# Scores of two column blocks in one two-bank PSUM piece, and the roots of the variances moved into the attention pairs

## The chip, the cores and the metric

The kernel runs on one core of one Trainium2 chip. The metric is the device time of one execution in microseconds (us). A core has a matrix engine (TensorE, rows named PE, and PEld for its weight loads), a vector engine (VectorE, DVE), a scalar engine (ScalarE, ACT), GpSimd (POOL) and SyncE (SP), which in this kernel issues every DMA. Each engine has a program of its own and works it off in the order in which it stands; engines meet at semaphores. PSUM, which takes the matmul results, has eight banks of 128 x 512 fp32 numbers.

## What is computed

One layer of an encoder is applied to 16 meta tokens with 512 prompt tokens and 1024 sample tokens (1552 columns in all, 1536 of them tokens). The lines that matter here:

```python
u = rms_norm(h, pre_g)
z = jnp.einsum('bld,de->ble', u, w_in.astype(u.dtype))
c_val, c_glu, c_gate, q, k, v, a_gate = jnp.split(z, [...], axis=-1)
conv_out = conv_module(c_val, c_glu, conv_w, conv_b, ln_g, ln_b) * jax.nn.silu(c_gate)
o_meta, o_grid = neighbourhood_attention(q[:, N_META:], k[:, N_META:], v[:, N_META:],
                                         q[:, :N_META], k[:, :N_META], v[:, :N_META], rel_bias)
att = jnp.concatenate([o_meta, o_grid], axis=1).reshape(B, L, D_ATT) * jax.nn.silu(a_gate)
mixed = jnp.concatenate([conv_out, att], axis=-1)
y = jnp.einsum('ble,ed->bld', mixed, w_out.astype(mixed.dtype))
return h + rms_norm(y, post_g)
```

`conv_module` ends in a layer norm over the 1024 channels of a token: `y = xc * lax.rsqrt(var + LN_EPS) * g + b`, and a silu. In the attention every query sees a window of 8 rows x 16 columns of the grid and the meta tokens: scores plus a relative bias, softmax, weighted values.

## The kernel before

Every matmul with weights is done three times, on a high and a low part of each operand (`hi`/`lo`, `qh`/`ql`, `kh`/`kl`, `mh`/`ml`). A scheduler inside the build sets the final order of each engine's program from the code's data flow; `tc.issue_after(x)` puts what stands in it behind `x`.

**Until about 660 us** the kernel normalises the tokens, projects values, gates and conv inputs, and runs the depthwise convolution, whose result goes to DRAM as `zs`.

**The attention** runs over 8 pairs of heads, 3 groups of token rows (`g`) and 2 halves (`hf`), so 48 steps of four column blocks `j` each: 192 blocks. In one turn of the loop `scores(p, g, hf)` stands for the step itself, `transposes` for the step before, `weighted` for the one before that, and `between` puts in a projection (`pair_proj`, `pair_q`, or in the last pair pieces of `a_gate`), 24 matmuls a piece into tiles `mm`. For a block `scores` has three matmuls into a tile `ss` (one PSUM bank of two, pool `ps_s`); VectorE adds the bias and takes the maximum out of it (L585, into `pt`), ScalarE takes the exponential (L589), VectorE the reciprocal and the scaling (L590, L591). `transposes` turns `pt` over on the matrix engine (`tp`, L600) and ScalarE copies it out (`pT`, L602); `weighted` sums the values into `po` (L616).

**Beside it** `statistics()` takes one call per step: it reads `zs`, and stores mean and variance of every token's 1024 channels to the DRAM tensor `std`. `roots()` then loads the 1536 variances into `rv` (128 x 12, L675), ScalarE takes the root (L676), VectorE the reciprocal (L677), and L678 stores them back, number by number:

```python
    s = std[1:2]
    var = bass.AP(s.tensor, s.offset, [[1, 128], [128, TG // 128]])
    nc.sync.dma_start(rv, var)
```

**The end:** `a_gate(6, 7)` (six pieces of 24 matmuls, copied out to `ag` by L342), then `mix(t, part)` makes the inputs of the last product for 128 tokens: part 0 loads mean and root (`mb`, L752), subtracts and multiplies on VectorE (L764, L765), silu on ScalarE (L767), times the silu of the gate (L768, L769), `mh` and `ml` (L770, L771); part 1 does the same for the attention. `load_wo` brings 16 chunks of the output weights (L735) and splits them (ScalarE L745, VectorE L746). `product` (L792) multiplies into `py`; tiles t = 0 and t = 1 are done together, part 0 of both first.

In the code before, `roots()` and the first `mix` stand behind the last pair:

```python
    with tc.issue_after(last_pt[0]):
        roots()
        mix(0, (0,))
```

Of the kernel before, what the change touches and what calls it, by code (L numbers as in the profile page):

```python
# [10 lines left out]
F32 = mybir.dt.float32  # L11
F32R = mybir.dt.float32r
AF = mybir.ActivationFunctionType
# [19 lines left out]
GR = (  # L33
    dict(R=9, k3=(0, 11, 0), k2=(0, 16, 0), vrow=0),
    dict(R=12, k3=(8, 12, 0), k2=(8, 16, 0), vrow=8),
    dict(R=13, k3=(13, 13, 0), k2=(10, 16, 3), vrow=13),
)
# [40 lines left out]
BMM, BSS, BTP = 3, 2, 2  # L78
# [15 lines left out]
def tile_encoder(ctx: ExitStack, tc: tile.TileContext, mt, xn, w_main, w_v, wo, cw, cb, lg, lb, pg, postg, rbt, rmask, y):  # L94
    nc = tc.nc
# [9 lines left out]
    const = ctx.enter_context(tc.tile_pool(name="const", bufs=1))  # L105
    es_ps = ExitStack()
    ps_mm = es_ps.enter_context(tc.tile_pool(name="ps_mm", bufs=BMM, space=bass.MemoryType.PSUM))
    ps_s = es_ps.enter_context(tc.tile_pool(name="ps_s", bufs=BSS, space=bass.MemoryType.PSUM))
    ps_t = es_ps.enter_context(tc.tile_pool(name="ps_t", bufs=BTP, space=bass.MemoryType.PSUM))
    ps_o = es_ps.enter_context(tc.tile_pool(name="ps_o", bufs=1, space=bass.MemoryType.PSUM))  # L110

    ones = const.tile([128, 128], F32, name="ones")
    nc.vector.memset(ones, 1.0 / D)
    eps_sb = const.tile([128, 3], F32, name="eps_sb")
# [4 lines left out]
    rv = const.tile([128, TG // 128], F32, name="rv")  # L119
# [311 lines left out]


    es2 = ExitStack()
    kpool = es2.enter_context(tc.tile_pool(name="kpool", bufs=1, side="right", reuse_waits="tile"))
    qpool = es2.enter_context(tc.tile_pool(name="qpool", bufs=1, side="right", reuse_waits="tile"))

# [14 lines left out]
    last = [None]  # L451
# [31 lines left out]
    last_qk = [None]  # L483
# [59 lines left out]
    def block(g, j):  # L543

        e = ebufs[g][{0: 1, 7: 2}.get(j, 0)]
        if g == 0:
            return min(max(j - 1, 0), 5), 3, "k3", 2, 108, e
        R8 = GR[g]["R"] * 8
        if j in (0, 7):
            return min(j, 6), 2, "k2", 2, R8, e  # L550
        return j - 1, 3, "k3", 3, R8, e

    def load_values(p, g):
        esl = slice(p * 128, p * 128 + 128)
        R8 = GR[g]["R"] * 8
        if g == 0:
            vt = apool.tile([108, 2, 6, 128], F32, name="vp", bufs=VPB)
            for ch, p0, b0, k0, n in ((0, 0, 0, 0, 72), (0, 72, 1, 0, 36), (1, 0, 1, 36, 36), (1, 36, 2, 0, 72)):
                nc.sync.dma_start(vt[p0:p0 + n, ch], vd[b0:b0 + 6, k0:k0 + n, esl].rearrange("b k e -> k b e"))
        else:  # L560
            vt = apool.tile([104, 8, 128], F32, name="vt", bufs=2)
            nc.sync.dma_start(vt[:R8], vd[:, GR[g]["vrow"] * 8:GR[g]["vrow"] * 8 + R8, esl].rearrange("b k e -> k b e"))
        vts[p, g] = vt

    def scores(p, g, hf):
        if hf == 0:
            load_values(p, g)
        kh, kl = kbufs[p]
        qh, ql = qbuf.pop((p, g, hf))
        R8 = GR[g]["R"] * 8  # L570
        for jj in range(4):
            j = hf * 4 + jj
            b0, nk, key, _, _, e = block(g, j)
            ra, rn, ro = GR[g][key]
            w = rn * 8
            ss = ps_s.tile([128, 512], F32, name="ss")
            for i, (q, k) in enumerate(((qh, kh), (qh, kl), (ql, kh))):
                last_qk[0] = nc.tensor.matmul(ss[:, :nk * w], lhsT=q[:, jj].rearrange("p h x -> p (h x)"),  # L578
                                 rhs=k[:, b0:b0 + nk, ra:ra + rn, :].rearrange("p b r c -> p b (r c)"),
                                 start=(i == 0), stop=(i == 2))  # L580
            sv_ = ss[:, :nk * w].rearrange("p (k x) -> p k x", k=nk)[:, :, ro * 8:ro * 8 + R8]
            pt = apool.tile([128, 312], F32, name="pt", bufs=PTB)
            pv = pt[:, :nk * R8]
            sm = apool.tile([128, 4], F32, name="sm", bufs=8)
            nc.vector.tensor_tensor_reduce(out=pv.rearrange("p (k x) -> p k x", k=nk), in0=sv_,  # L585
                                           in1=e.rearrange("p k r c -> p k (r c)"), scale=1.0,
                                           scalar=-3.0e38, op0=ALU.add, op1=ALU.max, accum_out=sm[:, 0:1])
            nc.vector.tensor_scalar(out=sm[:, 1:2], in0=sm[:, 0:1], scalar1=-1.0, scalar2=None, op0=ALU.mult)  # L588
            last[0] = nc.scalar.activation(out=pv, in_=pv, func=AF.Exp, bias=sm[:, 1:2], scale=1.0, accum_out=sm[:, 2:3])  # L589
            nc.vector.reciprocal(sm[:, 3:4], sm[:, 2:3])  # L590
            nc.vector.tensor_scalar(out=pv, in0=pv, scalar1=sm[:, 3:4], scalar2=None, op0=ALU.mult)  # L591
            pts[p, g, j] = pv
# [55 lines left out]
    def statistics():  # L648
        for t in range(TG // 128):
            tsl = slice(t * 128, t * 128 + 128)  # L650
            hx = []
            for k in range(2):
                x = gpool.tile([128, 512], F32, name="ag", tag="ag", bufs=2).rearrange("p (c t) -> p c t", c=8)
                a = t % 4 * 128 + k * 64
                nc.sync.dma_start(x, zs[t // 4][:, :, a:a + 64].rearrange("c p t -> p c t"))
                hx.append((x, slice(k * 64, k * 64 + 64)))
            yield
            for moment in range(2):
                for x, sl in hx:
                    nc.vector.tensor_reduce(out=ms[:, sl], in_=x.rearrange("p c t -> p t c"), op=ALU.add, axis=mybir.AxisListType.X)  # L660
                yield
                ps = new_mm()
                with tc.issue_after(last_mm[0]):
                    nc.tensor.matmul(ps[:, :128], lhsT=ones, rhs=ms, start=True, stop=True)
                nc.scalar.copy(out=row[0:1], in_=ps[0:1, :128])
                nc.sync.dma_start(std[moment:moment + 1, tsl], row[0:1])
                if moment == 0:
                    for x, sl in hx:
                        nc.vector.tensor_tensor(out=x, in0=x, in1=ps[:, sl].unsqueeze(1).broadcast_to([128, 8, 64]), op=ALU.subtract)
                        nc.scalar.activation(out=x, in_=x, func=AF.Square)  # L670

    def roots():
        s = std[1:2]
        var = bass.AP(s.tensor, s.offset, [[1, 128], [128, TG // 128]])
        nc.sync.dma_start(rv, var)  # L675
        nc.scalar.activation(out=rv, in_=rv, func=AF.Sqrt, bias=eps_sb[:, 1:2])  # L676
        nc.vector.reciprocal(rv, rv)  # L677
        nc.sync.dma_start(var, rv)  # L678

    stats = statistics()  # L680
    knext, last_pv, last_pt = [None], [None], [None]
# [2 lines left out]
    for n in range(len(groups) + 2):  # L684
        if n < len(groups):
            p, g, hf = groups[n]
# [67 lines left out]
    def mix(t, parts=(0, 1)):  # L754
        for part in parts:
            if part == 0:
                moments(t)
            mx, gt = mxs[part], gts[part]
            mh, ml = [x[t % 2 * 2 + part] for x in (mhs, mls)]
            g, csl = t // 4, slice(t % 4 * 128, t % 4 * 128 + 128)  # L760
            nc.sync.dma_start(mx, (zs, mad)[part][g][:, :, csl].rearrange("c p t -> p c t"))
            nc.sync.dma_start(gt, (cgd, agd)[part][g][:, :, csl].rearrange("c p t -> p c t"))
            if part == 0:
                nc.vector.tensor_tensor(out=mx, in0=mx, in1=mb[:, 0:1].broadcast_to([128, 8, 128]), op=ALU.subtract)  # L764
                nc.vector.tensor_tensor(out=mx, in0=mx, in1=mb[:, 1:2].broadcast_to([128, 8, 128]), op=ALU.mult)  # L765
                for c in range(8):
                    nc.scalar.activation(out=mx[:, c], in_=mx[:, c], func=AF.Silu, scale=lg_sb[:, c:c + 1], bias=lb_sb[:, c:c + 1])  # L767
            nc.scalar.activation(out=gt, in_=gt, func=AF.Silu)  # L768
            nc.vector.tensor_tensor(out=mx, in0=mx, in1=gt, op=ALU.mult)  # L769
            nc.scalar.copy(out=mh, in_=mx)  # L770
            (nc.vector if t < MLT else nc.gpsimd).tensor_tensor(out=ml, in0=mx, in1=mh.bitcast(F32), op=ALU.subtract)  # L771

    with tc.issue_after(last_pt[0]):
        roots()
        mix(0, (0,))
    for n in range(16):
        if n == 6:
# [132 lines left out]
```

## Time and profile before

| | |
|---|---|
| median of 3 runs | 1466.19 us (1464.93 to 4892.21) |
| the profiled execution | 1466.53 us, its span 1464.5 us |
| granted TensorE clock, mean | 0.996 of full speed |
| PE busy | 1436.8 us (98%) |
| DVE, ACT, POOL busy | 1014.2, 562.7, 256.6 us |

The span runs from the first to the last instruction; the execution's own time is 2.0 us longer. Times below are counted from the span's start. A matmul's end is modelled, so the distance from the start of one to the start of the next says more than its length.

### The profile page before, as it was taken

To read this page: it belongs to the slowest core of one execution; us is meant where nothing else is said; L and a number is where in the kernel's file an instruction comes from. 1 tells how busy PE (TensorE), PEld (TensorE's weight loads), DVE (VectorE), ACT (ScalarE), POOL (GpSimd) and SP (SyncE) were. 2 spreads that over 40 slices of the span, in tenths; PEclk is the share of its full clock that TensorE was granted. 3 is DMA by queue.
4 is the path that set the end of the run, shared out by engine and by line. 5 is a ranking of instruction groups with operands and counts; after the bars stand their busy time and mean duration, and the time that the engine had idled before them with its cause. 6 is when DMAs were issued, how large, how long until landed. Compare 5 with 4: busy or idle time off the path is not lost.

```text
span 1464.5 us, 24133 instructions
## 1 busy us (share of the span) xinstructions
PE 1436.8 (98%) x9536; PEld 1238.6 (85%) x9536; DVE 1014.2 (69%) x1739; ACT 562.7 (38%) x1298; POOL 256.6 (18%) x188
## 2 busy tenths in 40 slices
PE   7999999999999999999999999999999889999998
PEld 6988998988998888888888988988888768888886
DVE  6599999998999899836776777767543265332431
ACT  7311111112111111235565555655544465455440
POOL 2042022113101211222111111121110002122120
PEclk9999999999999999999999999999999989999999
DMA  8113113313231212242332232323232594545531
GB/s 267 42 47 118 47 55 110 93 40 91 74 97 51 88 59 87 94 116 65 87 88 80 69 98 77 88 79 89 72 93 81 130 312 135 167 122 148 160 107 43
DMA packets 153464, 145.19 MB, mean 99 GB/s; under 512 B 37216, under 2 KB 125432, under 8 KB 153352
## 3 DMA queue, kind: packets, MB, share of 16 engines
q1 hardware_dynamic: 153352, 143.67, 33.0%
q8 instruction: 74, 1.21, 0.3%
q14 instruction: 38, 0.31, 0.1%
HBM read 105.35 MB, written 42.72 MB: 101 GB/s over the span
## 4 chain that ended last, share of the span: by engine, by line
PE 92%; DMA 3%; ACT 2%; DVE 1%; POOL 1%; issue 1%; SPq 0%; DVEq 0%; ACTq 0%; POOLq 0%
PE mm L180 37%; PE py L792 18%; PE tp L180 9%; PE mm L322 5%; PE ss L578 5%; PE po L180 5%; PE po L616 4%; PE tp L600 4%; PE tp L322 3%; PE po L322 1%; POOL vl L142 1%; DMA std<-rv 1%; DMA yo<-in_wo 0%; ACT mx L767 0%; DMA wraw<-in_wo 0%
## 5 line engine op out<-in xcount | busy, mean ns | idle before, releaser
L180 PE MATMUL mm<-uw,whi 128*128 128x512 f32 (+2 forms) x1904 | 560.1, 371 | 3.3 <-ACT ag L342 3.3
L272 DVE SCALAR_TENSOR_TENSOR z<-ub,cw_sb,z 128x1536 f32<-128x1536 f32 (+2 forms) x270 | 498.7, 1853 | 8.1
L180 PEld LDWEIGHTS mm<-uw,whi 128*128 128x128 f32 x1904 | 341.8, 188 | 59.2 <-ACT ag L342 4.3
L180 PE MATMUL mm<-uw,wlo 128*128 128x512 f32 (+2 forms) x952 | 352.4, 370 | 1.1 <-POOL wlo L142 1.1
L142 POOL TENSOR_TENSOR wlo<-wraw,whi 128x1024 fp32r<-128x1024 f32 x48 | 130.5, 2720 | 524.3 <-ACT whi L141 500.3
L180 PEld LDWEIGHTS mm<-uw,wlo 128*128 128x128 f32 x952 | 179.0, 188 | 27.2 <-POOL wlo L142 1.4
L792 PE MATMUL py<-uw,mh 128*128 128x512 f32 x576 | 181.8, 397 | 0.0
L180 PE MATMUL tp<-uw,whi 128*128 128x512 f32 (+2 forms) x512 | 132.9, 344 | 0.0
L792 PEld LDWEIGHTS py<-uw,mh 128*128 128x128 f32 x576 | 108.7, 189 | 25.7
L589 ACT ACTIVATE pt<-pt,sm 128x216 f32<-128x216 f32 (+4 forms) x192 | 97.3, 507 | 80.3 <-DVE sm L588 70.3
L792 PE MATMUL py<-uw,ml 128*128 128x512 f32 x288 | 113.7, 396 | 0.0
L602 ACT COPY pT<-tp 108x256 f32<-108x256 f32 (+4 forms) x192 | 78.3, 420 | 84.5 <-PE tp L600 55.4
L764 DVE TENSOR_TENSOR mx<-mx,mb 128x1024 f32<-128x1024 f32 x12 | 14.7, 1225 | 123.2 <-DMA mx<-zs 107.8
L180 PEld LDWEIGHTS tp<-uw,whi 128*128 128x128 f32 x512 | 89.3, 188 | 11.6
L585 DVE CUSTOM_DVE_ANT_0 pt<-ss,ei 128x216 f32<-128x216 f32 (+2 forms) x144 | 62.6, 437 | 46.3 <-PE tp L600 22.7
L180 PE MATMUL tp<-uw,wlo 128*128 128x512 f32 (+2 forms) x256 | 88.1, 344 | 0.0
L771 POOL TENSOR_TENSOR ml<-mx,mh 128x1024 fp32r<-128x1024 f32 x20 | 48.4, 2443 | 224.2 <-ACT mh L770 224.2
L600 PE MATMUL tp<-ident,pt 128*96 128x128 f32 (+2 forms) x480 | 85.5, 275 | 0.3 <-ACT pT L602 0.2
L322 PE MATMUL mm<-vh,uw 128*128 128x256 f32 x448 | 83.5, 285 | 0.7 <-DVE uw L208 0.4
L591 DVE TENSOR_SCALAR pt<-pt,sm 128x216 f32<-128x216 f32 (+4 forms) x192 | 72.1, 375 | 4.9
L141 ACT CAST whi<-wraw 128x1024 fp32r<-128x1024 f32 x48 | 50.3, 1048 | 61.4 <-DMA wraw<-in_w_main 17.8
L180 PE MATMUL po<-uw,whi 128*128 128x512 f32 (+2 forms) x272 | 72.9, 347 | 0.0
(170 smaller groups left out, 2175.7 us busy)
## 6 DMA issues: line engine op xcount, KB each, us to landing
wraw<-in_w_main SPq DMA_DIRECT2D x48, 512.0 KB
xt<-in_xn SPq DMA_DIRECT2D x12, 512.0 KB
vd<-vs SPq DMA_DIRECT2D x96, 64.0 KB
zs<-zc SPq DMA_DIRECT2D x24, 256.0 KB
cgd<-ag SPq DMA_DIRECT2D x24, 256.0 KB
agd<-ag SPq DMA_DIRECT2D x24, 256.0 KB
ag<-zs SPq DMA_DIRECT2D x24, 256.0 KB
mad<-mo SPq DMA_DIRECT2D x24, 256.0 KB
```

Of the source, the lines that this page charges most:

```text
L142: eng.tensor_tensor(out=lo, in0=raw, in1=hi.bitcast(F32), op=ALU.subtract)
L180: last_mm[0] = nc.tensor.matmul(ps[:, :n], lhsT=w[:, dc, :], rhs=u[dc // 4][:, dc % 4, :], start=(dc == 0 and i == 0), stop=(dc == DC - 1 ...
L272: nc.vector.scalar_tensor_tensor(out=zv, in0=ub[:, a:b, k:k + 512], scalar=cw_sb[:, c, k:k + 1], in1=zv, op0=ALU.mult, op1=ALU.add)
L322: nc.tensor.matmul(ps[:, :256], lhsT=u[dc // 4][:, dc % 4, :], rhs=w[dc // 4][:, dc % 4, :], start=(dc == 0 and i == 0), stop=(dc == DC - ...
L578: last_qk[0] = nc.tensor.matmul(ss[:, :nk * w], lhsT=q[:, jj].rearrange("p h x -> p (h x)"), rhs=k[:, b0:b0 + nk, ra:ra + rn, :].rearrange ...
L585: nc.vector.tensor_tensor_reduce(out=pv.rearrange("p (k x) -> p k x", k=nk), in0=sv_, in1=e.rearrange("p k r c -> p k (r c)"), scale=1.0, ...
L589: last[0] = nc.scalar.activation(out=pv, in_=pv, func=AF.Exp, bias=sm[:, 1:2], scale=1.0, accum_out=sm[:, 2:3])
L591: nc.vector.tensor_scalar(out=pv, in0=pv, scalar1=sm[:, 3:4], scalar2=None, op0=ALU.mult)
L600: nc.tensor.transpose(out=tp[:kt, k * 128:k * 128 + 128], in_=pv[:, k * kt:k * kt + kt], identity=ident)
L602: last_pt[0] = nc.scalar.copy(out=pT[:kt, :nt * 128], in_=tp[:kt, :nt * 128]).ins
L616: last_pv[0] = nc.tensor.matmul(po[hs, j, :], lhsT=v, rhs=pT[:kt, k * 128 + h * 64:k * 128 + h * 64 + 64], start=(k == 0), stop=(k == nt - ...
L792: nc.tensor.matmul(pss[hf], lhsT=m[e // 8][:, e % 8], rhs=w[e][:, hf * 512:hf * 512 + 512], start=(n == 0 and i == 0), stop=(n == 15 and i ...
```

## The change

The two-bank pool `ps_s` is closed before the attention, and a pool `ps_ss` with a single piece of two banks takes its place. For every second block six matmuls fill both halves of the piece `sss`, first all of block j, then all of block j + 1; what follows for each block is as before. The next six wait until the piece has been read. The work of `roots()` goes to the end of `statistics()`: its load of `rv` is issued when the last variances are stored, in the seventh pair; the root comes two steps later, behind the exponential that was issued last there; the reciprocal and the store follow. `mix(0, (0,))` stays where it is in the code.

```diff
-    ps_s = es_ps.enter_context(tc.tile_pool(name="ps_s", bufs=BSS, space=bass.MemoryType.PSUM))
...
+    es_st = ExitStack()
+    ps_s = es_st.enter_context(tc.tile_pool(name="ps_s", bufs=BSS, space=bass.MemoryType.PSUM, reuse_waits="tile"))
...
+    es_st.close()
+    ps_ss = es_ps.enter_context(tc.tile_pool(name="ps_ss", bufs=1, space=bass.MemoryType.PSUM, reuse_waits="tile"))
...
+            if jj % 2 == 0:
+                sss = ps_ss.tile([128, 2, 512], F32, name="sss")
+                for y in range(2):
+                    b0, nk, key, _, _, e = block(g, j + y)
+                    ra, rn, ro = GR[g][key]
+                    for i, (q, k) in enumerate(((qh, kh), (qh, kl), (ql, kh))):
+                        last_qk[0] = nc.tensor.matmul(sss[:, y, :nk * rn * 8], lhsT=q[:, jj + y].rearrange("p h x -> p (h x)"),
+                                                      rhs=k[:, b0:b0 + nk, ra:ra + rn, :].rearrange("p b r c -> p b (r c)"),
+                                                      start=(i == 0), stop=(i == 2))
...
-            ss = ps_s.tile([128, 512], F32, name="ss")
-            for i, (q, k) in enumerate(((qh, kh), (qh, kl), (ql, kh))):
-                last_qk[0] = nc.tensor.matmul(ss[:, :nk * w], lhsT=q[:, jj].rearrange("p h x -> p (h x)"),
-                                 rhs=k[:, b0:b0 + nk, ra:ra + rn, :].rearrange("p b r c -> p b (r c)"),
-                                 start=(i == 0), stop=(i == 2))
+            ss = sss[:, jj % 2]
...
-    def roots():
         s = std[1:2]
         var = bass.AP(s.tensor, s.offset, [[1, 128], [128, TG // 128]])
         nc.sync.dma_start(rv, var)
-        nc.scalar.activation(out=rv, in_=rv, func=AF.Sqrt, bias=eps_sb[:, 1:2])
+        yield
+        yield
+        with tc.issue_after(last[0].ins):
+            nc.scalar.activation(out=rv, in_=rv, func=AF.Sqrt, bias=eps_sb[:, 1:2])
         nc.vector.reciprocal(rv, rv)
         nc.sync.dma_start(var, rv)
+        yield
...
     with tc.issue_after(last_pt[0]):
-        roots()
         mix(0, (0,))
```

The orders below are those of the built programs; line numbers of the changed kernel are a little higher than those of before (there L688 is the store of `rv`, L763 the load of `mb`, L775 and L776 the two steps of `mix` on VectorE, L593 to L599 the softmax, L582 the scores).

SyncE's DMA issues behind the last pair in the kernel before, where the roots are stored (`mad` and `agd` are stores of attention and gate, `xr` and `yo` take output weights):

```order
L343 DMA agd_68<-ag 128x512 [waits Activation_49]
L678 DMA std<-rv 128x12x1 [waits DMAHW1_49,DVE_49]
L621 DMA mad_65<-mo 128x512 [waits DMAHW2_49,DVE_49]
L752 DMA mb<-std 128x2x128 [waits DMAHW3_49,DMAHW1_49]
L735 DMA wraw<-in_wo 128x1024 [waits DMAHW4_49,Pool_49]
L735 DMA xr<-in_wo 128x1024 [waits DMAHW5_49,PE_49]
L735 DMA yo<-in_wo 128x1024 [waits DMAHW6_49,DMAHW2_49]
```

In the changed kernel these issues stand at the start of the eighth pair, ahead of the next gate's weights (`wraw<-in_w_main`) and of values (`vt`):

```order
L565 DMA vt<-vd 96x8x128 [waits DMAHW6_49,PE_49]
L629 DMA mad_64<-mo 128x512 [waits DMAHW7_49,DVE_49]
L688 DMA std<-rv 128x12x1 [waits DMAHW0_49,DVE_49]
L344 DMA agd_66<-ag 128x512 [waits DMAHW1_49,Activation_49]
L763 DMA mb<-std 128x2x128 [waits DMAHW2_49,DMAHW0_49]
L763 DMA mb<-std 128x2x128 [waits DMAHW3_49,DMAHW2_49,DVE_49]
L157 DMA wraw<-in_w_main 128x1024 [waits DMAHW4_49,Pool_49]
L565 DMA vt<-vd 104x8x128 [waits DMAHW5_49,PE_49]
```

The store of the roots and the first two loads of `mb` moved forward from behind the attention to the first steps of the eighth pair.

VectorE in the kernel before, at the same place of the program, behind the last softmax:

```order
L591 TENSOR_SCALAR pt<-pt,sm 128x208 [waits DVE_49]
L620 COPY mo<-po 128x512 [waits DMAHW0_49,PE_49]
L677 RECIPROCAL rv<-rv 128x12 [waits Activation_49]
L620 COPY mo<-po 128x512 [waits DMAHW6_49,DVE_49,PE_49]
L764 TENSOR_TENSOR mx<-mx,mb 128x1024 [waits DMAHW3_49]
L746 TENSOR_TENSOR wol_12185<-wraw,woh_12184 128x1024 [waits DMAHW4_49,Activation_49]
L765 TENSOR_TENSOR mx<-mx,mb 128x1024 [waits DVE_49]
```

VectorE in the changed kernel, from the last softmax of the seventh pair (216 columns: first blocks of the eighth):

```order
L599 TENSOR_SCALAR pt<-pt,sm 128x208 [waits DVE_49]
L687 RECIPROCAL rv<-rv 128x12 [waits Activation_49]
L593 ISA pt,sm<-sss,e_5367 128x216 [waits PE_49,Pool_49]
L593 ISA sm 128x1
L593 ISA pt,sm<-sss,ei_5366 128x216 [waits Pool_49]
L593 ISA sm 128x1
L596 TENSOR_SCALAR sm<-sm 128x1 [waits DVE_49] x2
L775 TENSOR_TENSOR mx<-mx,mb 128x1024 [waits DMAHW4_49,DMAHW2_49]
L598 RECIPROCAL sm<-sm 128x1 [waits Activation_49] x2
L776 TENSOR_TENSOR mx<-mx,mb 128x1024 [waits DVE_49]
L599 TENSOR_SCALAR pt<-pt,sm 128x216 [waits DVE_49] x2
L593 ISA pt,sm<-sss,ei_5366 128x216 [waits PE_49]
```

L775, which waits for `mx` and for `mb` (DMAHW2), moved between the first two blocks' maxima and the reads of the third and fourth block of the eighth pair.

The matrix engine in the kernel before, at the start of the eighth pair (264 columns) behind the last scores of the seventh (256):

```order
L578 MATMUL ss<-kh,ql_5357 128x256
L616 MATMUL po<-pT,vt 64x64 x22
L578 MATMUL ss<-kh,qh_5180 128x264 [waits DVE_49]
L578 MATMUL ss<-kl,qh_5180 128x264
L578 MATMUL ss<-kh,ql_5181 128x264
L578 MATMUL ss<-kh,qh_5180 128x264 [waits DVE_49]
L578 MATMUL ss<-kl,qh_5180 128x264
L600 MATMUL tp<-ident,pt 104x128 [waits Activation_49]
L600 MATMUL tp<-ident,pt 104x128 x2
L578 MATMUL ss<-kh,ql_5181 128x264
L180 MATMUL mm<-uw,whi 128x512
```

The matrix engine in the changed kernel, from the end of the second run of six of the eighth pair to the start of the third:

```order
L582 MATMUL sss<-kl,qh_5184 128x264
L582 MATMUL sss<-kh,ql_5185 128x264
L624 MATMUL po<-pT,vt 64x64 [waits DMAHW1_49]
L624 MATMUL po<-pT,vt 64x64 x21
L181 MATMUL mm<-uw,wlo 128x512
L181 MATMUL mm<-uw,whi 128x512
L582 MATMUL sss<-kh,qh_5190 128x264 [waits DVE_49,PE_49]
L582 MATMUL sss<-kl,qh_5190 128x264
L608 MATMUL tp<-ident,pt 104x128 [waits Activation_49]
```

Scores come in runs of six on one wait, where before each block of three waited for a bank of its own. Between the end of the first run of the eighth pair and the start of the third the changed program has 20 matmuls of a projection, 6 transposes, the 6 of the second run and 22 of `po`. In the whole attention it has the same 3598 matmuls; 14 of the 95 distances from one run of six to the next hold less than 1.5 us of other matmuls (at the distances from start to start of rows 8).

## Rows read from the trace of the kernel before

**Rows 1.** The page, busy time of each engine, share of the span, instructions.
```profile
PE 1436.8 (98%) x9536; PEld 1238.6 (85%) x9536; DVE 1014.2 (69%) x1739; ACT 562.7 (38%) x1298; POOL 256.6 (18%) x188
```

**Rows 2.** Waits of PE in the attention: total us, times, longest.
```profile
PE po L616 <- ACT pT L602: 0.5, 1, 0.5
PE tp L600 <- ACT pT L602: 0.2, 1, 0.2
```

**Rows 3.** Waits of PE from 1143 us to the end.
```profile
PE py L792 <- ACT mh L770: 4.6, 1, 4.6
PE mm L180 <- ACT ag L342: 3.3, 1, 3.3
PE py L792 <- ACT ag L342: 1.8, 1, 1.8
```

**Rows 4.** Windows: from:to, length, PE busy (matmuls), granted clock, DMA share, GB/s.
```profile
660.00:1142.00 482.00, 481.63 (x4338) 1.00 0.29 81
1142.00:1206.00 64.00, 53.92 (x222) 0.92 0.85 246
1202.00:1206.00 4.00, 4.00 (x11) 0.51 0.92 270
1206.00:1446.00 240.00, 240.00 (x1032) 1.00 0.45 134
```

**Rows 5.** Timeline of SyncE's issues: start, us, engine, line, what, [idle].
```profile
1144.28 0.37 SPq L678 DMA_DIRECT2D std<-rv  x1
1144.86 0.56 SPq L621 DMA_DIRECT2D mad<-mo  x1
1154.83 0.37 SPq L752 DMA_DIRECT2D mb<-std  x1
1155.29 0.42 SPq L735 DMA_DIRECT2D wraw<-in_wo  x1
```

**Rows 6.** Timeline of DVE behind the attention; in brackets idle time before, what ended it.
```profile
1144.03 0.23 DVE L677 RECIPROCAL rv<-rv 128x12 f32<-128x12 f32 x1 [15.05 <-ACT rv L676]
...
1160.17 1.23 DVE L764 TENSOR_TENSOR mx<-mx,mb 128x1024 f32<-128x1024 f32 x1 [15.34 <-DMA mb<-std]
1161.32 1.22 DVE L746 TENSOR_TENSOR wol<-wraw,woh 128x1024 fp32r<-128x1024 f32 x1
```

**Rows 7.** Timeline of ACT behind the attention.
```profile
1142.40 1.28 ACT L676 ACT_TABLE_LOAD   x1
1143.69 0.30 ACT L676 ACTIVATE rv<-rv,eps_sb 128x12 f32<-128x12 f32 x1
1144.01 1.28 ACT L768 ACT_TABLE_LOAD   x1
...
1161.38 1.05 ACT L745 CAST woh<-wraw 128x1024 fp32r<-128x1024 f32 x1 [14.08 <-DMA wraw<-in_wo]
...
1192.61 3.19 ACT L767 ACTIVATE mx<-mx,lb_sb,lg_sb 128x128 f32<-128x128 f32 x8
```

**Rows 8.** Timeline of PE late in the eighth pair.
```profile
1126.00 0.28 PE L578 MATMUL ss<-kl,qh 128*128 128x256 f32 x1
1126.12 0.28 PE L578 MATMUL ss<-kh,ql 128*128 128x256 f32 x1
1126.32 1.50 PE L616 MATMUL po<-pT,vt 96*64 96x64 f32 x44
1127.76 0.50 PE L180 MATMUL mm<-uw,whi 128*128 128x512 f32 x1
...
1129.02 0.49 PE L600 MATMUL tp<-ident,pt 128*104 128x128 f32 x3
1129.26 0.71 PE L180 MATMUL mm<-uw,whi 128*128 128x512 f32 x2
```

**Rows 9.** Timeline of PE and DVE around two scores' reads.
```profile
1097.62 0.29 PE L578 MATMUL ss<-kh,ql 128*128 128x288 f32 x1
1097.95 0.46 DVE L585 CUSTOM_DVE_ANT_0 pt<-ss,ei 128x288 f32<-128x288 f32 x1 [1.10 <-PE ss L578]
...
1122.23 0.47 DVE L585 CUSTOM_DVE_ANT_0 pt<-ss,ei 128x312 f32<-128x312 f32 x1
1122.63 0.09 DVE L585 DVE_READ_ACCUMULATOR2_ANT sm<- 128x1 f32 x1
1122.75 0.15 DVE L588 TENSOR_SCALAR sm<-sm 128x1 f32<-128x1 f32 x1
```

## The prediction

> **What bounds the kernel now.** I looked first at who is busy [rows 1]: the matrix engine is, 98% of the span, so only what makes it wait or run slower counts. Then at its waits by stage. In the attention it waits 0.7 us in 482 [rows 2, 4]: there the time is the sum of its own instructions, and an engine beside it matters only if it makes it wait. Behind the attention it waits 3.3, 1.8 and 4.6 us [rows 3]. The windows show the size of that hole: from 1142 to 1206 us PE is busy 53.9 of 64 us at a mean granted clock of 0.92, and within it there is a stretch at 0.51, so at the lower level of 1.2 GHz, right behind the longest wait [rows 4]. At the pace of the stage behind it, 240 us for 1032 matmuls or 0.2326 us each, its 222 matmuls take 51.6 us; 12.4 are lost, and since a few short `po` are among the 222 I say 13.
>
> The rows on SyncE, VectorE and ScalarE tell where the hole comes from. The store of the roots is issued at 1144.28, and the load of `mb`, which waits for it, at 1154.83 [rows 5]: SyncE stands 10 us before one landing, with the output weights behind it. VectorE idles 15.3 us until `mb` is there [rows 6] and ScalarE 14.1 us until output weights are [rows 7]. All the splitting of weights starts that much late and PE catches it up.
>
> **Scores in runs of six.** No matmul is added or taken away. What changes is a wait: the run after next to a read used to need one bank, now the next run needs both halves read. The first read of a block starts 0.33 us behind the start of the last score matmul, and from the start of a read to that of the next of its kind are about 0.5 us [rows 9], so a piece is free some 1.3 us behind its last matmul if VectorE comes at once. 14 of the 95 distances hold less than 1.5 us, the shortest about 0.5; at 0.1 to 0.5 us each that is 1 to 5 us of new waits, against at most the 0.7 that were there. I take 1.5, nearest to the read rows, as PE waited for no read before. With the 3598 matmuls the same, runs of six bring nothing back.
>
> **The roots leave the end.** Removed there are one table load and the root on ScalarE (1.6 us), one reciprocal, and SyncE's 10.5 us before the landing [rows 5 to 7]. ScalarE then has the weights 14 us earlier at most. What is late next is the silu and the cast of the first part of tile t = 1: in the old trace PE waited 4.6 us for that cast, until 1201.5 [rows 3]; its silu began at 1192.61 [rows 7]. With no wait PE gets there 198 matmuls behind the last `po` (six pieces of 24, then 54 of the product by the new order): 1142.8 + 198 x 0.2326 = 1188.9. The cast can come at 1187.4 at best (1201.5 less 14.1) and, if the 5 to 6 us that a load of weights takes from issue to cast there (1155.29 to 1161.38, [rows 5, 7]) hold half of it back, at 1194.5. So between 0 and 5.6 us of waiting stay; I take 3. The end gives 13 - 3 = 10 us, between 7 and 13.
>
> **The roots arrive in the attention**, and with them what hung on them. On ScalarE that is a table load to the root's set and one back to the exponential's, 1.28 us each, and 0.3 for the root [rows 7]; VectorE and PE have work of the step before, and I cost it at nothing, 2.9 us in the open if that cover were gone. The row shows the root starting 0.01 us behind its table load's end. The Trainium skill, "ScalarE: Activation LUTs", section "What ACT_TABLE_LOAD costs", counts a drain of about 1.38 us on top of 1.28 for every switch; the row shows none, and by that page the wait below would be 1.4 us longer and the time 1472.
>
> The price lies on VectorE. By the new order the first step of `mix` (L764 of old, now L775) stands there in the eighth pair, behind the reads of the first run of six and ahead of the softmax scaling of those blocks and of the reads of the second run. It waits for `mb`, `mb` for the store of the roots. Queued behind it is every further softmax; and PE's third run waits for the reads of the second. The third run's distance from the first is PE's cover: 20 projection matmuls (4.65 us), 6 transposes (0.33 for three with the slower matmul behind them, so 0.65), 6 scores at 0.12 (0.72) and the `po` at 1.44 [rows 4, 8], in sum 7.5 us. The store is issued somewhat before the first run ends: from the start of the table load to the issue were 1.9 us (1142.40 to 1144.28 [rows 5, 7]), the last softmax of the seventh pair reaches ScalarE about 3.5 us behind its scores by the order of reads and copies there, and the order puts 7.3 us of PE's work between these scores and the end of the first run; so about 1.2 us before it. Cover: 8.7 us.
>
> Needed are, from the store's issue: 10.55 to the issue of `mb` [rows 5]; 5.34 from there to VectorE's start (1154.83 to 1160.17 [rows 5, 6]); two steps of `mix` at 1.15 start to start [rows 6]; reciprocals and scalings of the two blocks, some 0.7; and the two reads, 1.0 [rows 9]. That is 19.9 us, so PE waits 19.9 - 8.7 = **11.2 us**. From below the bound is nothing, if both landings are quick; from above 12.5, if the second blocks' softmax backs up too. I take the full 11.2, since these are rows of the same two DMAs, with a 256 KB store issued beside the small one in both places (`mad` then [rows 5], `agd` now). SyncE is held too, by a second load of `mb` behind L776: weights and values in its queue go out some 17 us late, but the next weights wait for GpSimd, whose own turn comes later still, and the values are for the last group, so I cost that at nothing; if it were not, a wait of a few us in the same pair. Behind a wait of 4.6 us the clock stood at 0.51 with 11 matmuls in 4 us where 17 fit [rows 3, 4], 1.4 us lost; the same behind the longer wait, **1.5 us**.
>
> **Sum** against the profiled execution (1466.5, its span 1464.5 and 2.0 around it; 0.3 over the median): 1466.5 - 10 + 11.2 + 1.5 + 1.5 = 1470.7, so **1471**.
>
> **Rivals.** (a) *The landings in the attention are short.* If store and load together take under 4.7 us (8.7 of cover less the 4.0 that follow them), PE's third run comes without a wait, and the time is 1466.5 - 10 + 1.5 = **1458**. For it: the store is of 6 KB, and in the old place it ran into the last attention store. Against: 15.9 us in the rows. The Trainium skill, "DMA: Bandwidth & Descriptors", section "Anatomy of one DMA — SWDGE (gpsimd) path", fits about 2.0 us and bytes over 436 GB/s for a DMA, by which the two would take some 4.3 us and this rival would hold; the same section warns of long receipts when the target is HBM, and the row of 10.55 us stands on that side. Chance 0.17.
> (b) *The end gives nothing.* The order moves the roots, but if the loads of output weights were bound by buffers and not by SyncE's wait, the 13 us come back as waits for casts: 1466.5 + 11.2 + 1.5 + 1.5 = **1481**. For it: loads reuse two buffers in turn. Against: the first idle time of ScalarE ends right with the queue's release. Chance 0.1.
> (c) *The single piece makes every run wait.* PE runs six scores, VectorE takes 1.3 us or more for both reads, and with another 2.5 us of its queue before them even the usual distance (3.6 us) is not enough. It decides against the change from 0.31 us a run on, 95 x 0.31 = 29.4 us: **1500**, with the 1471 as base. For it: VectorE is busy 69% [rows 1] and its reads come in order with copies of up to 1.2 us. Against: PE waited for no read before. Chance 0.03.
>
> **How the numbers follow.** The forecast has 0.70. Its own range is 1466.5 + (-13 + 9 + 1) to 1466.5 + (-7 + 14 + 5), so 1463 to 1478; rival (a) reaches down to 1456, (b) up to 1482, and with these ends little over 1 in 10 is left out: **1456 to 1482**. A measurement of this kernel can tell about 2%, or 29 us, from no change; all but (c) lie within it: faster 0.01, same 0.96, slower 0.03.
>
> **What would show it.** Right: one wait of PE of about 11 us some 7 us behind the first scores of the eighth pair, ended by VectorE's read, with L775 idle before it for `mb`; the granted clock down at its end; SyncE's `mb` issue about 10.5 us behind the store; behind the attention no wait of ScalarE of 14 us, and PE's idle time there down from 10 us to about 3. Wrong: if `mb` lands within 5 us, if VectorE isn't idle before L775, or if waits of PE of some tenths stand before most runs of six. The largest unknown is the landing of the 1536 single numbers beside other traffic.

## The result, and the profile after

The changed kernel took 1474.67 us (median of 4 runs, 1473.66 to 1475.02) beside 1466.55 us for the kernel before: a ratio of 1.0056, 95% interval 1.0044 to 1.0069. That is 8 us more, within the 2% that count as no change. (One execution of the kernel before, at 4892 us, is a slow one and stands outside the ratio.) The profiled execution took 1474.38 us, its span 1472.3.

The page's busy line shows nothing new [rows 1], PE is busy 98% of a longer span:

```profile
PE 1437.4 (98%) x9536; PEld 1240.2 (84%) x9536; DVE 999.8 (68%) x1739; ACT 564.6 (38%) x1299; POOL 255.7 (17%) x188
```

PE's waits, from 660 to 1160 us and then from 1160 us to the end:

```profile
PE sss L582 <- DVE sm L593: 8.7, 1, 8.7
PE tp L608 <- ACT pT L610: 0.7, 1, 0.7
...
PE py L802 <- ACT ag L343: 8.1, 1, 8.1
```

There is one new wait in the attention, and behind it the 3.3, 1.8 and 4.6 us of before [rows 3] have become a single one of 8.1 us. So the hole at the end is not gone. The windows put sizes on both places (from:to, length, PE busy and matmuls, granted clock as a share of 2.4 GHz, DMA share, GB/s):

```profile
1074.00:1082.00 8.00, 0.00 (x0) 0.68 0.07 19
1082.00:1087.00 5.00, 4.70 (x17) 0.50 0.10 26
1087.00:1092.00 5.00, 5.00 (x32) 0.99 0.33 107
1188.00:1196.00 8.00, 0.04 (x1) 0.81 0.91 312
1196.00:1200.00 4.00, 4.00 (x10) 0.53 1.02 395
...
1154.00:1218.00 64.00, 55.92 (x257) 0.95 0.80 259
1218.00:1458.00 240.00, 240.00 (x1032) 1.00 0.44 130
```

The clock fell to the lower level while PE stood, and stayed there some 5 us after it went on, at half the pace: about 2.4 us lost. The 64 us from 1154 hold 257 matmuls, against 222 of before [rows 4], but some 22 of the 257 are short `po`; counted from the last `po`, 64 us hold 234 matmuls of projections and product, against 217.

The first wait, followed from SyncE to VectorE to PE (timelines; in brackets the idle time before and what ended it):

```profile
1064.44 0.36 SPq L688 DMA_DIRECT2D std<-rv  x1
1064.90 0.67 SPq L344 DMA_DIRECT2D agd<-ag  x1
1075.29 6.17 SPq L763 DMA_DIRECT2D mb<-std  x2
1087.36 0.35 SPq L157 DMA_DIRECT2D wraw<-in_w_main  x1
```

```profile
1078.58 1.23 DVE L775 TENSOR_TENSOR mx<-mx,mb 128x1024 f32<-128x1024 f32 x1 [11.52 <-DMA mb<-std]
1079.86 1.21 DVE L776 TENSOR_TENSOR mx<-mx,mb 128x1024 f32<-128x1024 f32 x1
```

```profile
1073.24 0.40 PE L181 MATMUL mm<-uw,whi 128*128 128x512 f32 x1
1082.30 0.56 PE L582 MATMUL sss<-kh,qh 128*128 128x264 f32 x1 [8.66 <-DVE sm L593]
...
1187.49 0.39 PE L181 MATMUL mm<-uw,whi 128*128 128x512 f32 x1
1195.96 0.80 PE L802 MATMUL py<-woh,mh 128*128 128x512 f32 x1 [8.08 <-ACT ag L343]
```

`mb` is issued 10.85 us behind the store of the roots (10.55 before [rows 5]), VectorE stands 11.5 us at L775, and PE's third run of six waits for the reads that stand behind it. The last two rows are the second wait: PE has finished the last projection and cannot begin the first product, whose PSUM bank ScalarE has not emptied. On ScalarE:

```profile
1062.56 1.28 ACT L686 ACT_TABLE_LOAD   x1
1063.85 0.30 ACT L686 ACTIVATE rv<-rv,eps_sb 128x12 f32<-128x12 f32 x1
...
1188.19 0.57 ACT L343 COPY ag<-mm 128x512 f32<-128x512 f32 x1
1188.77 1.06 ACT L779 ACTIVATE gt<-gt 128x1024 f32<-128x1024 f32 x1
1190.23 1.04 ACT L756 CAST uw<-wraw 128x1024 fp32r<-128x1024 f32 x1 [0.41 <-DMA wraw<-in_wo]
1192.75 1.04 ACT L756 CAST uw<-xr 128x1024 fp32r<-128x1024 f32 x1 [1.47 <-DMA xr<-in_wo]
1194.38 1.04 ACT L756 CAST uw<-yo 128x1024 fp32r<-128x1024 f32 x1 [0.59 <-DMA yo<-in_wo]
1195.33 0.58 ACT L343 COPY ag<-mm 128x512 f32<-128x512 f32 x1
```

The copy of the last projection's result (1195.33) stands in ScalarE's queue behind a silu and three casts, and the casts wait for loads of output weights (idle times in brackets).

Two marks divide the difference: the start of the last `po`, and the rest of the span. The last `po` came at 1142.66 before and comes at 1154.49 now, +11.8; from there to the end of the span 321.8 us became 317.9, -4.0. Together 7.8, the difference of the spans. (The stretch from the last `po` to the 193rd product matmul, of which the expectations below speak, differs by the same 4.0: 92.0 and 88.0 us; behind it all kernels run alike, 229.8 us each.)

### The profile page after: what moved, and what is told of

Same layout as the page of the kernel before. It is cut to its first block, busy times and chain, and to the rows that moved or that the text cites. A ratio compares the mean times of both kernels' runs of the same rounds, so it can differ in the third digit from the quotient of the medians.

```text
span 1472.3 us, 24133 instructions
## 1 busy us (share of the span) xinstructions
PE 1437.4 (98%) x9536; PEld 1240.2 (84%) x9536; DVE 999.8 (68%) x1739; ACT 564.6 (38%) x1299; POOL 255.7 (17%) x188
## 4 chain that ended last, share of the span: by engine, by line
PE 91%; DMA 4%; DVE 2%; ACT 1%; POOL 1%; issue 0%; DVEq 0%; SPq 0%; ACTq 0%; POOLq 0%
PE mm L181 36%; PE py L802 18%; PE tp L181 9%; PE mm L323 5%; PE po L181 5%; PE sss L582 5%; PE po L624 4%; PE tp L608 3%; PE tp L323 3%; DMA wraw<-in_wo 1%; PE po L323 1%; POOL vl L143 1%; DMA std<-rv 1%; DMA ag<-zs 1%; DMA yo<-in_wo 0%
## 5 line engine op out<-in xcount | busy, mean ns | idle before, releaser
L593 DVE CUSTOM_DVE_ANT_0 pt<-sss,ei 128x216 f32<-128x216 f32 (+2 forms) x144 | 60.0, 437 | 77.6 <-PE sss L582 76.1
L181 PEld LDWEIGHTS tp<-uw,whi 128*128 128x128 f32 x512 | 89.3, 188 | 11.6
L775 DVE TENSOR_TENSOR mx<-mx,mb 128x1024 f32<-128x1024 f32 x12 | 15.1, 1256 | 121.2 <-DMA mx<-zs 109.7
L608 PE MATMUL tp<-ident,pt 128*96 128x128 f32 (+2 forms) x480 | 82.1, 275 | 0.7 <-ACT pT L610 0.7
L499 ACT ACTIVATE qh<-mm 64x256 fp32r<-64x256 f32 x96 | 36.2, 378 | 98.6 <-PE sss L582 67.0
```

Of the source, the lines that this page charges most:

```text
L181: last_mm[0] = nc.tensor.matmul(ps[:, :n], lhsT=w[:, dc, :], rhs=u[dc // 4][:, dc % 4, :], start=(dc == 0 and i == 0), stop=(dc == DC - 1 ...
L608: nc.tensor.transpose(out=tp[:kt, k * 128:k * 128 + 128], in_=pv[:, k * kt:k * kt + kt], identity=ident)
```

## The experiments

My theory at first: VectorE's wait for `mb` behind a slow landing makes the loss in the attention, and the move of the roots all of the difference. The rivals: the runs of six cost something themselves; SyncE's standing costs. The expectations of scores alone, roots alone, contiguous store and mix held were written together, before any of them ran. That a shared bank is the missing gain at the end came out of the first two, with a rival of its own: the weights' loads set the end whatever the bank. All measured, ratios with 95% intervals, each to executions of the kernel before on the same chip (medians 1466.6 to 1466.7 us):

| kernel | median us | ratio to before | last `po` | rest of the span |
|---|---|---|---|---|
| before | 1466.6 | | 1142.66 | 321.8 |
| changed | 1474.67 | 1.0056 [1.0044, 1.0069] | 1154.49 | 317.9 |
| scores alone | 1471.69 | 1.0035 [1.0023, 1.0047] | 1142.64 | 326.5 |
| roots alone | 1467.90 | 1.0011 [1.0002, 1.0020] | 1156.65 | 312.1 |
| changed, contiguous store | 1464.78 | 0.9985 [0.9977, 0.9994] | 1142.92 | 319.6 |
| changed, mix held | 1461.12 | 0.9966 [0.9954, 0.9979] | 1143.31 | 317.3 |
| changed, other bank | 1469.21 | 1.0017 [1.0008, 1.0026] | 1154.16 | 313.2 |
| scores alone, other bank | 1466.21 | 0.9997 [0.9988, 1.0006] | 1142.75 | 321.0 |
| changed, contiguous, other bank | 1458.78 | 0.9946 [0.9934, 0.9959] | 1142.72 | 314.1 |
| changed, held, other bank | 1455.88 | 0.9929 [0.9916, 0.9941] | 1143.13 | 310.8 |
| before, contiguous store | 1458.55 | 0.9943 [0.9930, 0.9956] | 1143.08 | 314.0 |
| changed, held, other bank, early mix | 1452.40 | 0.9901 [0.9885, 0.9917] | 1142.57 | 307.7 |

**Scores alone.** The roots go back behind the last pair (`roots()` as before, called ahead of `mix(0, (0,))`); pools and runs of six as in the changed kernel.

> The scores in runs of six and one piece of two banks, the roots left at the end. Theory (the move of the roots makes all of the difference: 8.7 us of waiting and 2.4 us of half clock in the attention, less 4.0 given back at the end): within 1.5 us of the kernel before, 1465 to 1468 us, and all of PE's waits in the attention together under 1.5 us. Rival (the single piece carries part of the loss, since a run needs both banks read): 1470 us or more, with waits for the reads of the piece in many runs.

Neither: the time is the rival's, 1471.69 us, but not by its mechanism. The waits from 660 us on:

```profile
PE py L800 <- ACT ag L343: 8.8, 1, 8.8
PE mm L181 <- ACT ag L343: 4.1, 1, 4.1
PE tp L608 <- ACT pT L610: 0.7, 1, 0.7
```

No run of six waits, and the last `po` comes at the same time as before to 0.02 us. All of the 5 us lie behind the attention, where this part of the change has no instruction. This run changed my theory.

**Roots alone.** `scores` and the pools as before, the roots in the statistics.

> The roots in the statistics as in the changed kernel, the scores in two single banks as before. Theory: VectorE's wait for mb stops the reads here too, PE waits 7.5 to 9 us for a bank in the eighth pair, the clock falls for some 10 us, the end gives back about 4: 1472 to 1475 us. Rival (only the single piece lets that wait through to PE, two banks of their own hide it): no wait above 2 us in the attention, 1461 to 1465 us.

```profile
PE ss L578 <- DVE sm L585: 9.1, 2, 8.9
PE py L794 <- ACT mh L773: 2.5, 1, 2.5
...
```

The wait in the attention is as the theory has it, two single banks do not hide it. But the time is 1467.90 us, under its 1472 to 1475: the end gives back 9.7 us (312.1 beside 321.8), not 4. With the last `po` at 1156.65, of which 2.4 us are an execution that came later to its first score already (649.38 us; before, 646.98), the attention loses 11.6, so a net of +1.9 beside the measured 1.3.

So the 4 us of the changed kernel are this 9.7 less what the scores' part costs at the end (4.65 alone). What does it change there? The built programs show it. The first `py` takes bank 0. The six projections behind the attention take, one after another, banks 0, 2, 1, 0, 2, 1 in the kernel before and in roots alone, so bank 0 was last used by the third projection from the end. In the changed kernel, and in scores alone, they take 1, 2, 0, 1, 2, 0, so it was last used by the last one. In the kernel before PE went on at the copy of that third projection from the end (the 1.8 us of [rows 3]):

```profile
1180.81 0.58 ACT L342 COPY ag<-mm 128x512 f32<-128x512 f32 x1
1181.45 0.50 PE L792 MATMUL py<-woh,mh 128*128 128x512 f32 x1 [1.79 <-ACT ag L342]
```

The place of the pool does not do this. The change opens `ps_s` last, which moves the transposes and `po` to other banks; but the kernel before, built with `ps_s` opened last, keeps 0, 2, 1 for the projections, and so does the changed kernel built with its own pools and, as before, three matmuls into each of two single banks. It is the runs of six that turn the sequence, within the attention, from the 97th of the 173 tiles `mm` on. (These two kernels were built and not run; why the runs of six turn it is not followed here.)

**The bank.** To undo just that, the last of the six projections takes a bank of the transposes:

```diff
     with tc.issue_after(last_pv[0]):
-        for _ in a_gate(6, 7):
-            pass
+        banks[:] = 0, ((ps_mm, "mm"),) * 5 + ((ps_t, "tp"),)
+        for _ in a_gate(6, 7): pass
```

> The changed kernel with the last of the six projections behind the attention put into a bank of the transposes, so that the bank of the first product (py) was last used by the third of the six; the order is the same on every engine. Theory (the end gave back 4 us instead of 10 because the new order of the pools lets the first py share a bank with the last projection, whose copy stands in ScalarE's queue behind casts of output weights): the wait of 8.1 us before the first py goes; PE comes to the first product of t = 1 at 1187.9 + 54 x 0.2326 = 1200.4, its cast ends at 1203.7, so a wait of 2 to 4 us takes its place: 1468 to 1471 us. Rival (casts and loads of the output weights set the end, whatever the bank): the waits at the end sum up to 8 us again, 1473 to 1476 us.

> The scores alone (roots at the end, runs of six, one piece) with the last projection in a bank of the transposes. Theory: all that the scores' change costs is the shared bank; without it the wait of 8.9 us before the first py becomes the waits of the kernel before (1.8 and 4.6 us), 1465 to 1468 us. Rival (something else in the scores' change costs the 5 us): 1470 to 1473 us.

1469.21 and 1466.21 us, both times as the theory has them. (The waits that are left in scores alone are not quite those it named: 4.8 us for a projection's bank and 3.5 us for the cast of t = 1, 8.3 in sum beside 9.7 before [rows 3].) The changed kernel's waits with this bank:

```profile
PE sss L582 <- DVE sm L593: 8.9, 1, 8.9
PE py L802 <- ACT mh L781: 3.8, 1, 3.8
...
```

The wait for the copy is gone, the cast of t = 1 takes its place at 3.8 us. Scores alone become the kernel before (0.9997), so the bank was all that they cost, and the runs of six themselves cost nothing that can be measured.

**Contiguous store.** `rv` becomes 12 partitions of 128 numbers, in columns that the statistics no longer need:

```diff
-    ms, row = spare[:, 0:128], spare[:, 128:256]
+    ms, row, rv = spare[:, 0:128], spare[:, 128:256], spare[:TG // 128, 0:128]
...
-        var = bass.AP(s.tensor, s.offset, [[1, 128], [128, TG // 128]])
+        var = bass.AP(s.tensor, s.offset, [[128, TG // 128], [1, 128]])
...
-            nc.scalar.activation(out=rv, in_=rv, func=AF.Sqrt, bias=eps_sb[:, 1:2])
+            nc.scalar.activation(out=rv, in_=rv, func=AF.Sqrt, bias=eps_sb[:TG // 128, 1:2])
```

> The changed kernel with the roots worked out on 12 partitions of 128 numbers, so that their store writes 12 rows of 512 bytes instead of 1536 single numbers; the order of instructions is the same on every engine. Theory (the wait is the landing of single numbers): the statistics' own 512-byte stores let the next instruction go 1.1 us behind their issue (1026.85 to 1027.93), so mb is issued 1 to 3 us behind the store instead of 10.85, L775 waits 3 to 5 us instead of 11.5, PE's wait of 8.7 falls under 1.5 us and the half clock goes with it: 1462 to 1465 us. Rival (the store stands behind the 256 KB stores issued before and beside it, whatever its shape): mb still 9 us or more behind the store, 1473 to 1475 us.

SyncE, then VectorE:

```profile
1064.52 0.32 SPq L688 DMA_DIRECT2D std<-cw_sb  x1
1064.94 0.33 SPq L344 DMA_DIRECT2D agd<-ag  x1
1065.82 6.33 SPq L763 DMA_DIRECT2D mb<-std  x2
```

```profile
1069.26 1.23 DVE L775 TENSOR_TENSOR mx<-mx,mb 128x1024 f32<-128x1024 f32 x1 [2.93 <-DMA mb<-std]
```

`mb` follows the store by 1.30 us instead of 10.85, with the same order on every engine and the same 256 KB store beside it. VectorE waits 2.9 us, PE not at all, and the attention ends where it did before. 1464.78 us; the rival is out. The end still has the shared bank (9.1 us of waiting).

The store's shape also shows in the transfers. The DMA view of 1063 to 1077 us in 40 slices (busy share in tenths, then GB/s), first the changed kernel, then the contiguous store:

```profile
DMA  9899999999999999490992109000003020000020
GB/s 284 208 298 285 255 297 334 251 33 244 118 111 35 23 35 53 6 35 0 18 18 6 6 0 35 0 0 6 6 6 18 6 35 12 6 0 0 0 79 20
```

```profile
DMA  9999930198021123300000000000333210000000
GB/s 303 282 293 297 338 117 24 41 386 322 1 85 51 50 70 95 92 0 0 0 0 0 0 0 0 0 0 3 88 89 88 79 28 0 0 0 0 23 0 0
```

In the changed kernel the bytes trickle from 1068.6 on, at 35 GB/s or less, until about 1075.0, where `mb` is released: of 1601 packets of 4 bytes all but 16 start before 1067, but the 2 KB packets of the gate's store (`agd`) take up to 4.7 us each, and the last of both kinds end together. With the contiguous store the same 2 KB packets take at most 0.14 us and end at 1066.55. The store of single numbers holds up the store beside it as well.

**Mix held.** The first mix is put behind the last copy of the attention's result on VectorE (`last_mo[0]`); the roots and their slow store stay:

```diff
...
-    with tc.issue_after(last_pt[0]):
+    with tc.issue_after(last_pt[0]), tc.issue_after(last_mo[0]):
         mix(0, (0,))
```

> The changed kernel with the first mix (on VectorE: L775 onward) held behind the last copy of the attention's results, the roots and the first load of mb where they are. Theory (VectorE standing for mb is what stops PE): no wait of PE over 1 us in the eighth pair though mb's load is as late as ever, last po about 11 us earlier than 1154.5, the end as long as in the changed kernel (88 us from the last po to the 193rd product matmul, 92 at most): 1462 to 1467 us. Rival (SyncE standing 10.9 us behind the store, with weights and values in its queue, is what costs): a wait of similar size for weights or values, 1471 us or more.

```profile
1064.35 0.36 SPq L688 DMA_DIRECT2D std<-rv  x1
...
1075.48 0.36 SPq L763 DMA_DIRECT2D mb<-std  x1
```

```profile
1144.19 1.22 DVE L775 TENSOR_TENSOR mx<-mx,mb 128x1024 f32<-128x1024 f32 x1
```

```profile
PE py L802 <- ACT ag L343: 7.5, 1, 7.5
PE tp L608 <- ACT pT L610: 0.7, 1, 0.7
```

SyncE stands 11.1 us behind the store as in the changed kernel, and PE does not wait there (the two lines are all its waits from 660 us on; the longer is that for the shared bank): 1461.12 us, just under the theory's 1462. It is VectorE's place in the order that costs, not SyncE's 11 us. The second load of `mb`, behind which SyncE stood too, goes with L776 to the end, so this run does not show what that one costs. The order at the end changes as well, and the rest of the span is 0.6 us shorter.

**Both repairs together.** The other bank with the contiguous store, and with the held mix:

> The changed kernel with the contiguous store of the roots and the last projection in a bank of the transposes. Theory: the two gains add up as far as the cast of t = 1 allows: PE comes to t = 1 at 1176.3 + 12.6 = 1188.9, the cast ends at 1193.1, so 9.05 us of waiting become about 4: 1458 to 1461 us. Rival (the end is bound by weights): 1463 to 1465 us, as without the other bank.

> The changed kernel with the first mix held behind the attention and the last projection in a bank of the transposes. Theory: the wait of 7.5 us before the first py becomes one of about 3 us for the cast of t = 1 (due at 1192.8, PE there at about 1190): 1455 to 1458 us. Rival (the end is bound by weights): 1459 to 1463 us, as without the other bank.

1458.78 and 1455.88 us, within both forecasts of the theory. What is left are waits of 3.2 and 2.8 us for the cast of t = 1.

**Was the move needed?** The kernel before with the contiguous store alone:

> The kernel before, roots at the end and scores as they were, but the roots worked out on 12 partitions of 128 numbers, so that their store writes 12 rows of 512 bytes. Theory (what the roots cost at the end was the landing of single numbers, so the store's shape gives back what the move gave back, without a place in the attention): mb is issued 1 to 3 us behind the store instead of 10.5, the stretch from the last po to the 193rd product matmul falls from 92.0 to 83 to 86 us as in the kernel with the roots alone moved (82.3), 1458 to 1462 us. Rival (at the end the store lands late behind the attention's last stores whatever its shape): 1465 to 1468 us.

```profile
1145.52 0.32 SPq L678 DMA_DIRECT2D std<-cw_sb  x1
1146.06 0.33 SPq L621 DMA_DIRECT2D mad<-mo  x1
1146.48 0.38 SPq L735 DMA_DIRECT2D wraw<-in_wo  x1
1146.96 0.41 SPq L752 DMA_DIRECT2D mb<-std  x1
```

1458.55 us: with the other shape of the store, at the roots' old place, the end gives back 7.8 us, without a place in the attention. The order behind the attention is not that of before, on any of PE, VectorE, ScalarE and SyncE (a load of weights stands ahead of `mb`), so how much of the 7.8 is the landing alone is not separated; that `mb` follows the store by 1.44 us instead of 10.55 is.

**The last wait.** In the held kernel with the other bank, `mix(1, (0,))` loses its `tc.issue_after(last_copy[0])`, so that its silu may stand ahead of the last copies on ScalarE:

> The changed kernel with the first mix held behind the attention, the last projection in a bank of the transposes, and the mix of tile t = 1 no longer held behind the last copy of a projection on ScalarE. Theory (the last wait at the end, 2.8 us, is for the cast of t = 1, whose silu stands behind that copy in ScalarE's queue): no wait above 1 us behind the attention, 1452 to 1454.5 us. Rival (the casts of the output weights then come that much later and PE waits for them): 1455 to 1458 us, as with the copy in front.

```profile
660.00:1142.00 482.00, 481.27 (x4328) 1.00 0.30 81
1142.00:1206.00 64.00, 64.00 (x302) 1.00 0.85 277
```

1452.40 us, 0.990 of the kernel before and the fastest here. The 64 us from 1142 that held 222 matmuls at the start [rows 4] now hold 302 without a wait; counted from the last `po`, without the short ones, 277 beside 217.

## Why the prediction was right, and where its terms were off

The time (1474.7 beside 1471 forecast) and the sign were right, and in the attention the path was the one described; the end was not, for a reason that the prediction had not seen. That the sum came so near is in part luck: against the forecast the end gave 6.0 us less, the wait in the attention cost 2.5 less, the half clock 0.9 more, the runs of six 1.5 less there, and 0.8 us of the 11.8 in the attention belong to none of the terms.

**What bounds the kernel** held: in every kernel PE's waits, and half of the time that it ran at the lower level, give the change up to the last `po` and that behind it to within 0.6 us each, but for the 2.4 us by which roots alone came late to its first score.

**Runs of six, 1.5 us.** Measured: 0.0 in the attention. My 14 short distances did not bite, and were miscounted: in the changed kernel's trace 3 of the 95 are shorter than 1.5 us from the start of a run's last matmul to the start of the next run, the shortest 1.2. But the sentence "What changes is a wait" was the step that failed. The runs of six also turn the sequence in which the projections take their banks; that costs 4.65 us at the end (scores alone, the profiled execution) and vanishes with the bank (scores alone, other bank). [rows 3] had the clue, a wait of the first `py` for a copy, which I took as part of the hole and never followed to its bank.

**The end, -10 us.** By itself this term was right: roots alone give back 9.7. In the changed kernel it is -4.0, since the first `py` now waits 8.1 us for the last copy. I had named the cast of t = 1 as what is late next; it is so only once the bank is repaired (3.8 us in the changed kernel, my 3 plus 0.8).

**The wait in the attention, 11.2 us.** Right place, right releaser, 8.66 us. The store's landing is as forecast (10.85 for 10.55). Too long was the step from `mb`'s issue to VectorE, taken from the old place at 5.34 us: here 3.29 (1075.29 to 1078.58). What follows on VectorE took 3.72 for 4.0, and the cover was 9.2 for 8.7 (1064.44 to 1082.30 less 8.66). Held mix shows that VectorE's standing carries it all, and that SyncE's 11 us behind the store cost nothing. Its second standing, costed at nothing too, was not taken away by itself; in the changed kernel the next weights go out at 1087.36, right behind GpSimd's turn (1084.96 and 2.38 us), as I had put it, and PE waits for none of them.

**The half clock, 1.5 us.** Measured some 2.4: PE ran at the lower level for 4.8 us, not 3.

**Rival (a)**, short landings, was wrong for this store and right for its condition: with the contiguous store, store and load together take 4.74 us (1064.52 to 1069.26), PE waits for nothing there, and with the bank repaired the time is 1458.8, where (a) forecast 1458. That number is luck in part: (a) has -10 for the end and 1.5 for the runs of six, where -7.7 (314.1 beside 321.8) and 0 were measured. The Trainium skill, "DMA: Bandwidth & Descriptors", section "Anatomy of one DMA — SWDGE (gpsimd) path", fits about 2.0 us and bytes over 436 GB/s to a DMA on GpSimd's path, while SyncE issues every DMA here; measured, the same 6 KB take 1.30 us to the issue of `mb` as 12 rows and 10.85 as 1536 numbers, so that constant fits neither. In the Trainium skill the section "Why small descriptors are slow (HBM only)" of the same page names a fixed cost of every packet, which points the right way; whether it is what acts here, no run shows. **Rival (b)**, an end that gives nothing, is out by roots alone. **Rival (c)**, every run waiting, is out by scores alone. The drain that the Trainium skill's "ScalarE: Activation LUTs", section "What ACT_TABLE_LOAD costs", counts on top of a table load does not show here either: the root starts 0.01 us behind the load's end (1062.56 + 1.28 to 1063.85).

What stays open: the two parts alone cost 1.3 and 5.1 us, 6.4 in sum, against 8.1 together. The shared bank is not the reason: it costs 5.5 us by itself (1471.69 to 1466.21) and in the changed kernel (1474.67 to 1469.21), and with the other bank the parts cost 0.8 in sum against 2.5 together. Some of it is the wait for the cast of t = 1, 3.8 us with both parts and 2.5 with the roots alone; what makes that cast later was not followed.

## What to carry to other kernels

When a diff changes the order of the matmuls, look at which tiles share a bank afterwards, far from the edit: the first user of a bank inherits the queue of the engine that empties it last (8.1 us here). Before moving a slow step to where it might be hidden, ask why it is slow: here the shape of a 6 KB store cost 9.6 us of landing, and mending it in place brought 8 us, where the move by itself lost 1.3. And an instruction moved early waits in its engine's queue with all that stands behind it; hold it behind the work that must not wait, even if its data are fetched early.

## What the runs showed of the hardware

In nine kernels with a store of 1536 single numbers, the load that waits for it was issued 10.5 to 11.4 us behind it, at both places and beside different traffic. The same bytes in rows of 512 took 1.30 and 1.65 us, and 1.44 at the end (1145.52 to 1146.96), though other DMAs were issued between.

Beside the single numbers the 256 packets of 2 KB of the stores next to it took 0.41 us on average (changed kernel, 1063 to 1077 us), beside the rows 0.09.

The granted clock did not go by the length of a wait. In the kernel before PE waits 3.3 us until 1163.0 and 1.8 us until 1181.5 [rows 3]; the windows up to 1182 us and behind it (length, then busy time of PE, its weight loads, VectorE, ScalarE and GpSimd, granted clock, DMA share, GB/s):

```profile
1142.00:1182.00 40.00, 34.48 (x154) 27.59 (x155) 16.11 (x15) 18.21 (x27) 2.38 (x1) 1.00 0.75 200
1182.00:1186.00 4.00, 4.00 (x12) 3.12 (x11) 3.79 (x5) 3.18 (x4) 0.00 (x0) 0.57 0.90 262
```

Behind the longer wait the clock stayed at the upper level. A mean of 0.57 means 3.4 of the 4 us at the lower level (0.43 / 0.5 x 4), behind the shorter. What decides is not shown here.
